# A hybrid layer's weight splits: one queue with steps four ticks apart, and row sums of a block loaded ahead

## The chip, the core and the metric

The kernel runs on one core of one Trainium2 chip. The metric is the device time of one execution in microseconds, the median of several runs. One further execution is recorded by the hardware profiler; all durations below that are called "profiled" come from it.

## The reference

One layer of a generator over 2048 tokens of width 1024, with 256 context tokens ahead of it. An input projection of 9216 columns feeds eight heads of a gated linear recurrence in both directions (query, value, two forget gates, output gate) and a gated short convolution of 1024 channels; one output projection follows, and a residual add and a norm.

```python
h = rmsnorm(x, norm_w[l]) * (1.0 + scale[:, None]) + shift[:, None]
p = h @ w_in[l]                                     # 2048 x 1024 @ 1024 x 9216
pc = hc @ (w_in[l, :, :HG_COLS] if last else w_in[l])   # 256 context rows, recurrence columns only
qc, vc, kcf, gcf, kcb, gcb = hgrn_prep(pc[..., :HG_COLS], lb_f, lb_b)
oc, s_f, s_b = bidir_scan(qc, kcf, kcb, vc, gcf, gcb, s0, s0)
q, v, kf, gf, kb, gb = hgrn_prep(p[..., :HG_COLS], lb_f, lb_b)
o, _, _ = bidir_scan(q, kf, kb, v, gf, gb, s_f, s_b)
y_hg = hgrn_out(o, p[..., 4 * HG_WIDTH:HG_COLS], hg_onorm_w[l], x.dtype)
y_cv = conv_branch(p[..., HG_COLS:], conv_w[l], grid=True)
y = jnp.concatenate([y_hg, y_cv], axis=-1) @ w_out[l]
```

`bidir_scan` runs the recurrence S_t = diag(f_t) S_{t-1} + k_t v_t^T, o_t = S_t^T q_t forwards and backwards. All of it is float32, so the kernel carries every matmul operand as two float16 parts, a high one and the remainder.

## The kernel before

**Units.** The input projection goes by *pairs* of 128 weight columns. A pair and a group of 512 tokens make a *unit* (`seven`, lines 881 to 925): seven products A11·B11, S1·T1, S2·T2, A12·B21, S3·T3, S4·B22, A22·T4 on half-size operands, each of three matmuls (high·high, high·low, low·high) in each of four steps. After every such step of three matmuls stands a *tick* (line 1372). A unit has 28 ticks. Its products collect in three PSUM banks, in the trace `sa`, `sb` and `sc`; ScalarE copies `sa`, `sb`, `sa` out after the first three products (`keep`, line 897), VectorE adds the later ones (`plus`, line 901). The last product, A22, is issued within the next unit, after that one's first.

**Order of work.** Each of eight heads has four windows of 512 tokens. A window has a unit of the *z pair* (the two gates' columns; p24 to p31 in names are the z pairs of heads 0 to 7), a unit of the *v pair* (value and query; p8 to p15), and in some windows a unit of a *gate pair* shared by two heads (p32, p34, p36, p38, with buffers of its own, `own=True`). The first window of a head has short context units too (8 ticks each). Then come four windows of the first convolution pairs (p56 and p48) and fourteen windows of pairs p57 to p63 and p49 to p55, in which a unit is 512 columns wide instead of 256. In between, at ticks set by a table of paces, stand the steps of the recurrence: multiplications of K, Q and tot by levels on VectorE, copies on ScalarE, small matmuls.

**Splitting a pair.** `load_pair` (line 364) makes the operands of a pair from two staged blocks of 128 x 1024 float32. Row sums: `sizes` (line 378, ScalarE, two activations) and their sum `rb` (382). `begin` (385) calls `pow2_scale`, which puts one 128x1 matmul `ss` on TensorE (line 139) that reads `rb`, and three tiny VectorE instructions that make the scale `sc`. Then come the splits (lines 151 and 152: ScalarE casts the high part, VectorE computes the remainder) of A11 with A12 in one instruction of 1024, of S1, A22, S2, S3, S4 in 512 each, and VectorE sums at 393, 404, 410 and 413 that make S1 to S4 in place.

**When it is split.** When the last use of a pair is over, `retire` calls `next_w(own, 4)`. It takes the block loaded ahead, or loads one, empties whatever of older pairs is still to be split (`flush`), and puts the new pair into `deferred` with a wait of four ticks. From then on `tick` (1372 to 1379) takes one step of the front pair at each tick: the two row sums, a gap of six ticks in the heads or two in the convolution (line 415), then the nine steps from `begin` to S4 at nine ticks in a row, and last a load of the next block (`load_ahead`). `settle` at a unit's start (line 1390) issues what is left of that unit's pair.

**What sets the order on an engine.** The program's order gives each instruction its priority; a scheduler then fills each engine's queue from what is ready by its own account. A step may so stand earlier in a queue than its tick says, and never waits for its tick on the chip: only the place in the queue counts, and each engine runs its queue in order.

## Time and profile before

| | us |
|---|---|
| median of 3 runs | 2182.38 |
| lowest and highest run | 2182.03, 2183.33 |
| the profiled execution | 2187.49 |
| its span, first to last instruction | 2185.7 |
| TensorE busy in the span | 2089.4 |
| VectorE busy | 1652.1 |
| ScalarE busy | 1169.2 |
| granted TensorE clock, mean | 0.99 |

The profiled execution took 1.8 us more than its span, and 5.1 us more than the median of the runs. A busy engine is one with an instruction in work; for TensorE the difference between span and busy time, 96 us, is the time in which it waited.

### The profile page before, as it was taken

Reading aid. Unit: us, or ns where it says so; the run is one execution under the profiler, and the core shown is the slowest. Engines: PE = TensorE matmul, PEld = TensorE weight load, DVE = VectorE, ACT = ScalarE, POOL = GpSimd, SP = SyncE. Lnnn points to the kernel's source line nnn. Section 1 sums busy time; section 2 is a strip of 40 time slices with the busy share of each in tenths; the row PEclk is TensorE's granted clock in tenths of the full one; section 3 lists DMA queues with packets and bytes.
Section 4 is the critical chain, followed back from the end, with each engine's and each line's share of the span. In section 5 each row is a group of like instructions: output and inputs, shape, how many; then the busy total and the mean of one; then the engine's idle time right before and its main releaser. Section 6 shows DMA issues by size and latency. Waiting matters only on the chain.

```text
span 2185.7 us, 51899 instructions
## 1 busy us (share of the span) xinstructions
PE 2089.4 (96%) x21563; PEld 1468.2 (67%) x21563; DVE 1652.1 (76%) x3456; ACT 1169.2 (53%) x2341; POOL 157.9 (7%) x239
## 2 busy tenths in 40 slices
PE   5789999999999999999999999999999999999998
PEld 2677688888887988888889887444444444444443
DVE  7887777878779778788687786677787656687775
ACT  7865556666557565666675654344444423333332
POOL 0211111010010110101111000000000000000000
PEclk9999999999999999999999999999999999999999
DMA  9766533433243333333633448923443205633321
GB/s 349 238 205 208 181 132 103 141 116 105 86 159 107 114 114 125 111 108 128 194 123 123 140 156 260 274 97 121 135 139 98 66 30 181 213 124 108 127 85 58
DMA packets 196464, 310.41 MB, mean 142 GB/s; under 512 B 13570, under 2 KB 126594, under 8 KB 194436
## 3 DMA queue, kind: packets, MB, share of 16 engines
q1 hardware_dynamic: 194068, 303.16, 42.5%
q8 instruction: 169, 2.77, 0.5%
q10 hardware_dynamic: 2160, 3.93, 0.5%
q14 instruction: 67, 0.55, 0.1%
HBM read 241.77 MB, written 65.27 MB: 140 GB/s over the span
## 4 chain that ended last, share of the span: by engine, by line
PE 66%; DVE 18%; ACT 8%; DMA 5%; issue 2%; POOL 1%; SPq 0%; POOLq 0%; ACTq 0%; DVEq 0%
PE sa L890 8%; PE sa L891 8%; PE sa L892 8%; PE sb L890 4%; PE sb L891 4%; PE sb L892 4%; PE sa_o L890 2%; PE sa_o L891 2%; PE sa_o L892 2%; DVE e_p L152 2%; PE A L599 2%; PE sc L890 2%; PE sc L892 2%; PE sc L891 2%; DVE K L453 2%
## 5 line engine op out<-in xcount | busy, mean ns | idle before, releaser
L453 DVE TENSOR_TENSOR K<-K,tot 128x512 f32<-128x512 f32 x192 | 133.6, 696 | 60.1 <-PE A L627 27.6
L891 PEld LDWEIGHTS <-e_p 128*128 128x128 f16 x1368 | 134.1, 98 | 60.4 <-issue 10.9
L890 PEld LDWEIGHTS <-e_p 128*128 128x128 f16 x1368 | 134.1, 98 | 59.9 <-DMA hop1T<-Hd1T 2.6
L892 PEld LDWEIGHTS <-e_p 128*128 128x128 f16 x1368 | 134.2, 98 | 52.8 <-issue 1.8
L460 DVE TENSOR_TENSOR Q<-Q,tot 128x512 f32<-128x512 f32 x192 | 132.4, 690 | 44.3 <-PE A L599 30.9
L569 ACT ACTIVATE km<-K 128x512 f32<-128x512 f32 x160 | 109.0, 686 | 69.5 <-DVE K L453 60.0
L890 PEld LDWEIGHTS <-whib_p 128*128 128x128 f16 x912 | 89.3, 98 | 41.2 <-issue 5.0
L890 PEld LDWEIGHTS <-whia_p 128*128 128x128 f16 x912 | 89.4, 98 | 38.5 <-DMA hop3B<-Hd3B 2.8
L891 PEld LDWEIGHTS <-whib_p 128*128 128x128 f16 x912 | 89.4, 98 | 38.2 <-issue 4.1
L891 PEld LDWEIGHTS <-whia_p 128*128 128x128 f16 x912 | 89.3, 98 | 37.7 <-issue 5.6
L892 PEld LDWEIGHTS <-wlob_p 128*128 128x128 f16 x912 | 89.4, 98 | 34.7 <-issue 0.5
L892 PEld LDWEIGHTS <-wloa_p 128*128 128x128 f16 x912 | 89.4, 98 | 34.4
L151 ACT ACTIVATE e_p<-ws_p,sc_p 128x512 f16<-128x512 f32 x108 | 77.2, 717 | 53.4 <-DVE ws_p L413 33.3
L576 POOL COPY qm<-Q 128x512 f32<-128x512 f32 x64 | 55.7, 870 | 630.2 <-DVE Q L460 627.2
L635 POOL COPY A<-Ac 32x128 f32<-32x128 f32 x128 | 68.3, 534 | 371.2 <-ACT A L631 367.2
L897 ACT ACTIVATE u<-sa,sx_w 128x256 f32<-128x256 f32 (+1 forms) x114 | 59.8, 525 | 59.2 <-PE sa L892 48.7
L897 ACT ACTIVATE p<-sb,sx_w 128x256 f32<-128x256 f32 (+1 forms) x114 | 59.4, 521 | 52.9 <-PE sb L892 52.3
L897 ACT ACTIVATE p<-sa,sx_w 128x256 f32<-128x256 f32 (+1 forms) x114 | 59.1, 518 | 47.4 <-PE sa L892 46.6
L152 DVE SCALAR_TENSOR_TENSOR e_p<-ws_p,sc_p,e_p 128x512 f16<-128x512 f32 x108 | 78.5, 742 | 1.0 <-ACT e_p L151 1.0
L813 ACT ACTIVATE cv<-c,small 128x512 f32<-128x512 f32 (+1 forms) x36 | 24.2, 674 | 97.6 <-DVE c L831 52.9
L378 ACT ACTIVATE junk<-ws_p 128x1024 f16<-128x1024 f32 x72 | 75.7, 1051 | 0.2
L151 ACT ACTIVATE hiS_o<-y_o,sc_y 128x1024 f16<-128x1024 f32 x32 | 36.8, 1149 | 72.6 <-PE sa_o L891 32.2
(865 smaller groups left out, 6972.1 us busy)
## 6 DMA issues: line engine op xcount, KB each, us to landing
ws_p<-in_w_in SPq DMA_DIRECT2D x72, 512.0 KB, 4.4
y_o<-yT SPq DMA_DIRECT2D x32, 512.0 KB, 4.2
xt_x<-in_x SPq DMA_DIRECT2D x16, 512.0 KB, 4.6
wa<-in_w_ada SPq DMA_DIRECT2D x16, 512.0 KB, 10.2
Gd<-zs SPq DMA_DIRECT2D x32, 256.0 KB, 3.2
...
```

Of the source, the lines that this page charges most:

```text
L151: S.activation(hi, src, AF.Copy, scale=st[:, 0:1])
L152: V.scalar_tensor_tensor(lo, src, st[:, 0:1], hi, ALU.mult, ALU.subtract)
L378: S.activation(junk.rearrange("p (k n) -> p k n", k=KT), stage[i], AF.Abs, accum_out=r)
L453: V.tensor_tensor(m, m, sub(cur, nb + 1, [[2, np_], [-(nb + 1), 2], [0, B]]), ALU.mult)
L460: V.tensor_tensor(m, m, sub(cur, 1, [[2, np_], [nb - 1, 2], [0, B]]), ALU.mult)
L569: S.activation(sub(s.km, 0, [[2 * B, n // (2 * B)], [B, 2], [1, B]]), mix(s.K, n, B, n // (2 * B)), AF.Copy)
L576: G.tensor_copy(sub(qm, 0, [[2 * B, n // (2 * B)], [B, 2], [1, B]]), mix(s.qf, n, B, n // (2 * B)))
L635: G.tensor_copy(A3[js, :, js], s.Ac[js])
L890: PE.matmul(ps, hi[:, k], rh, start=start and k == 0, stop=False, skip_group_check=not start)
L891: PE.matmul(ps, hi[:, k], right(name, 1, k), start=False, stop=False, skip_group_check=not start)
L892: PE.matmul(ps, lo[:, k], rh, start=False, stop=k == nk - 1, skip_group_check=not start)
L897: last_keep.append(S.activation(r, ps, AF.Copy, scale=sx))
```

## The change

`deferred`, a list of pairs with their steps, becomes `jobs`, a queue of generators. A tick counts down the wait of every job, and moves the front job alone by one step when its wait is over; a job that is finished leaves the queue. Nothing empties the queue any more but `settle`, and that only up to the pair that the unit needs.

- A pair's steps are parted into `pre` (the two row sums) and `rest` (the nine steps from `begin` to S4). Between two steps of `rest` stand `room` ticks: 4 for the heads' pairs, 3 and 2 for the first two convolution blocks, 1 after that.
- When a block has been loaded ahead, a job of its own is queued with a wait of 16 ticks, which takes its row sums two ticks apart. It stands behind the splits of the pair in front. When that pair's turn comes, its `pre` is empty, and it goes to `begin` without the gap.
- A gate pair is loaded when its job comes to the front (not when the older one retires), and 12 ticks later its row sums begin. The first gate pair, p32, so goes from `begin` at the fourth tick of window 1's z unit, with a step at every tick, to `begin` at the sixteenth tick, with one at every fourth.

The same instructions are issued; the changed kernel's line numbers are one higher from line 417 on (its copies of products are at 898). Matmuls of the products are untouched. By ticks, the nine steps of a z pair stay in the last window's v unit and the start of the gate unit behind it; those of the v pair move from the gate unit to the gate unit's end and the next head's first z unit; those of the gate pairs p34, p36 and p38 move from that z unit to the first v unit and the second window.

```diff
--- before.py
+++ after.py
@@ -412,10 +412,11 @@
         def sum_b():
             V.tensor_tensor(a12, a12, a11, ALU.subtract)
 
-        gap = 6 if col0 < 5 * HG else 2
-        w.rest = [lambda: behind(lambda: sizes(0)), lambda: behind(lambda: sizes(1))] + [lambda: None] * gap
-        w.rest += [begin, whole, part("S1", lambda: t["s1"]), sum_a, part("A22", lambda: a22),
-                   part("S2", lambda: a11), sum_b, part("S3", lambda: a21), part("S4", lambda: a12)]
+        w.pre = [lambda: behind(lambda: sizes(0)), lambda: behind(lambda: sizes(1))]
+        w.rest = [begin, whole, part("S1", lambda: t["s1"]), sum_a, part("A22", lambda: a22),
+                  part("S2", lambda: a11), sum_b, part("S3", lambda: a21), part("S4", lambda: a12)]
+        block = col0 // P - 5 * HEADS
+        w.gap, w.room = (6, 4) if block < 0 else (2, {0: 3, 1: 2}.get(block % 8, 1))
         return w
 
 
@@ -961,15 +962,13 @@
         load_C(ext.op, 0, OPS[6:])
         load_C(ext.op, 1, OPS)
 
-    deferred = []
-
-    def settle(w):
-        while w.rest:
-            w.rest.pop(0)()
-
-    def flush():
-        while deferred:
-            settle(deferred.pop(0)[1])
+    jobs = []
+
+    def settle(wk):
+
+        while any(j_[1] == wk for j_ in jobs):
+            for _ in jobs.pop(0)[2]:
+                pass
 
     def wo_scan(k):
         for j in range(2):
@@ -1266,6 +1265,8 @@
     ws = {}
 
     ahead, loaded = [], []
+    given = [0, 0]
+    in_order = [list(todo[0]), list(todo[1])]
 
     def load(own):
         wk = todo[own].pop(0)
@@ -1277,17 +1278,44 @@
 
         if todo[0] and not ahead and not loaded[-2].rest:
             ahead.append(load(0))
+            jobs.append([16, None, sizes_ahead(ahead[0])])
+
+    def sizes_ahead(w):
+        while w.pre:
+            w.pre.pop(0)()
+            yield
+            yield
+
+    def split_steps(own):
+
+        if ahead and not own:
+            w = ahead.pop()
+        else:
+            w = load(own)
+            yield from range(12)
+        load_ahead()
+        if w.pre:
+            while w.pre:
+                w.pre.pop(0)()
+                yield
+            yield from range(w.gap)
+        while w.rest:
+            w.rest.pop(0)()
+            yield from range(w.room)
+        load_ahead()
 
     def next_w(own, wait=0):
-        if todo[own] or (ahead and not own):
-            flush()
-            w = ahead.pop() if ahead and not own else load(own)
-            if wait:
-                w.rest.append(load_ahead)
-                deferred.append([wait, w])
-                load_ahead()
-            else:
-                settle(w)
+        if given[own] == len(in_order[own]):
+            return
+        wk = in_order[own][given[own]]
+        given[own] += 1
+        if wait:
+            jobs.append([wait, wk, split_steps(own)])
+        else:
+            w = load(own)
+            for f_ in w.pre + w.rest:
+                f_()
+            w.pre, w.rest = [], []
 
 
     hop = {}
@@ -1371,12 +1399,12 @@
 
         def tick(weight):
             pace[0] += weight
-            for d_ in deferred:
-                d_[0] -= 1
-            while deferred and not deferred[0][1].rest:
-                deferred.pop(0)
-            if deferred and deferred[0][0] <= 0:
-                deferred[0][1].rest.pop(0)()
+            for j_ in jobs:
+                j_[0] -= 1
+            if jobs and jobs[0][0] <= 0:
+                front = jobs[0]
+                if next(front[2], front) is front:
+                    jobs.remove(front)
             while not pending and pace[1] < len(steps) and steps[pace[1]][0] * total <= pace[0]:
                 steps[pace[1]][1]()
                 pace[1] += 1
@@ -1386,8 +1414,8 @@
             gw -= 1
         turnover = wi + 1 < len(group_of) and group_of[wi + 1] != group_of[wi]
         for un, (wk, kind, i, fn) in enumerate(units):
+            settle(wk)
             w = ws[wk]
-            settle(w)
             if not hasattr(w, "sx"):
                 finish_w(w, f"w{ui}")
             final = turnover and kind != "ctx" and all(u[1] == "ctx" for u in units[un + 1:])
```

**Head 1 to head 2, z pair p26, TensorE.** `ss_p26` is the scale's matmul; `sb`, `sc` and `sa` are products of the running unit, `A4` and `A5` small matmuls of the recurrence. Before:

```order
L892 MATMUL sc_26_5287<-hop7B21_4815,wloa_p9_3299 128x256
L139 LDWEIGHTS rb_p26_5268
L139 MATMUL ss_p26_5300<-rb_p26_5268 128x1
L617 MATMUL A5_1_1_5313<-Q_1_1_4972,K_1_1_4481 32x64 x16
L890 LDWEIGHTS e_p9_3302
L890 MATMUL sa_26_5166<-hop7T3_4848,e_p9_3302 128x256
```

After:

```order
L893 MATMUL sb_26_5210<-hop7T1_4513,wlob_p9_3325 128x256
L139 LDWEIGHTS rb_p26_3619
L139 MATMUL ss_p26_5227<-rb_p26_3619 128x1
L600 MATMUL A4_1_1_5240<-qm3_1_1_5191,km3_1_1_5145 32x32 x16
L600 MATMUL A4_1_1_5240<-Q_1_1_4978,km4_1_1_5194 32x32 x16
L891 LDWEIGHTS e_p9_3326
L891 MATMUL sa_26_5172<-hop7T2_4759,e_p9_3326 128x256
```

It stood behind the product A12 (`sc_26`) and stands behind S1 (`sb_26`), two products earlier, ahead of the S2 product (`sa_26<-hop7T2`).

**The same place, ScalarE.** `rsum` are p26's row sums, `whia`, `whib` and `e` the high parts of its splits, `p1`, `p5` and `u2` copies of products, `f`, `K` and `km` the recurrence. Before, ahead of the first split:

```order
L378 ACTIVATE junk_129,rsum_p260_5221<-ws_p260_3194 128x1024
L491 ACTIVATE f_1_0_4942<-f_1_0_4942,lb_136,lb1_137 128x512
L510 ACTIVATE f_1_0_4942<-sa_25_4944,sx_w16_3368 128x256
L492 ACTIVATE K_1_0_4943<-f_1_0_4942 128x512
L491 ACTIVATE f_1_0_4942<-f_1_0_4942,lb_136,lb1_137 128x512
L897 ACTIVATE p5_26_5261<-sb_26_5208,sx_w19_3715 128x256
L492 ACTIVATE K_1_0_4943<-f_1_0_4942 128x512
L378 ACTIVATE junk_129,rsum_p261_5266<-ws_p261_3196 128x1024
L897 ACTIVATE u2_26_5285<-sa_26_5166,sx_w19_3715 128x256
L569 ACTIVATE km0_1_0_5650<-K_1_0_4943 128x512
```

The row sums after the change stand in the first window of head 1, a head earlier:

```order
L898 ACTIVATE u2_16_3477<-sa_16_3358,sx_w16_3353 128x256
L378 ACTIVATE junk_129,rsum_p260_3609<-ws_p260_3312 128x1024
L378 ACTIVATE junk_129,rsum_p261_3617<-ws_p261_3314 128x1024
L512 ACTIVATE f_1_3_3356<-f_1_3_3356 128x256
L570 ACTIVATE km4_0_3_3602<-K_0_3_2633 128x512
```

and the splits:

```order
L493 ACTIVATE K_1_0_4949<-f_1_0_4948 128x512
L492 ACTIVATE f_1_0_4948<-f_1_0_4948,lb_136,lb1_137 128x512
L898 ACTIVATE p5_26_5278<-sb_26_5210,sx_w19_3721 128x256
L493 ACTIVATE K_1_0_4949<-f_1_0_4948 128x512
L151 ACTIVATE whia_p26_5233<-ws_p260_3312,sc_p26_5229 128x1024
L151 ACTIVATE whib_p26_5235<-s1_p26_5238,sc_p26_5229 128x512
L898 ACTIVATE u2_26_5301<-sa_26_5172,sx_w19_3721 128x256
L151 ACTIVATE whib_p26_5235<-ws_p261_3314,sc_p26_5229 128x512
L151 ACTIVATE e_p26_5237<-ws_p261_3314,sc_p26_5229 128x512
L570 ACTIVATE km0_1_0_5636<-K_1_0_4949 128x512
L151 ACTIVATE e_p26_5237<-ws_p260_3312,sc_p26_5229 128x512
L898 ACTIVATE p1_27_5420<-sa_27_5370,sx_w9_1688 128x256
```

The two row sums have left this place, and copies of products now stand between the splits.

**Head 2, gate pair p34, VectorE.** `wloa`, `wlob` and `e` are remainders, `ws` and `s1` the sums in place, `f_2_0` outputs of the z unit, `vT_2_0` and `q_2_0` of the v unit, `Q`, `K`, `Ac`, `ks` and `S` steps of the recurrence. Before, in the z unit:

```order
L460 TENSOR_TENSOR Q_1_0_5420<-Q_1_0_5420,tot_1_0_5648 128x64x2x4
L152 SCALAR_TENSOR_TENSOR wloa_p34_5744<-ws_p340_5625,sc_p34_5739,whia_p34_5743 128x1024
L152 SCALAR_TENSOR_TENSOR wlob_p34_5746<-s1_p34_5748,sc_p34_5739,whib_p34_5745 128x512
L410 TENSOR_TENSOR ws_p340_5625<-s1_p34_5748,ws_p340_5625 128x512
L152 SCALAR_TENSOR_TENSOR wlob_p34_5746<-ws_p341_5627,sc_p34_5739,whib_p34_5745 128x512
L413 TENSOR_TENSOR ws_p340_5625<-ws_p340_5625 128x512
L152 SCALAR_TENSOR_TENSOR e_p34_5747<-ws_p340_5625,sc_p34_5739,e_p34_5747 128x512
L607 COPY_PREDICATED Ac_1_0_5710<-mask_138,A2_1_0_5788 128x128
L152 SCALAR_TENSOR_TENSOR e_p34_5747<-ws_p341_5627,sc_p34_5739,e_p34_5747 128x512
L607 COPY_PREDICATED Ac_1_0_5710<-mask_138,A2_1_0_5788 128x128
L152 SCALAR_TENSOR_TENSOR e_p34_5747<-ws_p340_5625,sc_p34_5739,e_p34_5747 128x512
L901 SCALAR_TENSOR_TENSOR f_2_0_5593<-sb_28_5631,sx_w28_5590,u2_28_5722 128x256
```

After, in the v unit:

```order
L454 TENSOR_TENSOR K_1_0_4949<-K_1_0_4949,tot_1_0_5634 128x4x2x64
L461 TENSOR_TENSOR Q_1_0_5416<-Q_1_0_5416,tot_1_0_5634 128x4x2x64
L152 SCALAR_TENSOR_TENSOR wloa_p34_6026<-ws_p340_5858,sc_p34_6021,whia_p34_6025 128x1024
L902 SCALAR_TENSOR_TENSOR vT_2_0_5956<-sc_31_6036,sx_w31_5953,p1_31_5984 128x256
L152 SCALAR_TENSOR_TENSOR wlob_p34_6028<-s1_p34_6030,sc_p34_6021,whib_p34_6027 128x512
L902 SCALAR_TENSOR_TENSOR q_2_0_5957<-sa_31_5958,sx_w31_5953,p5_31_6005 128x256
L410 TENSOR_TENSOR ws_p340_5858<-s1_p34_6030,ws_p340_5858 128x512
L152 SCALAR_TENSOR_TENSOR wlob_p34_6028<-ws_p341_5860,sc_p34_6021,whib_p34_6027 128x512
L902 SCALAR_TENSOR_TENSOR vT_2_0_5956<-sb_31_5986,sx_w31_5953,u2_31_6034 128x256
L538 TENSOR_TENSOR ks_2_0_6158<-K_2_0_5579 128x512
L696 SCALAR_TENSOR_TENSOR S_1_0_3_6121<-S_1_1_0_5487,tot7_1_0_5635,T_1_01_6116 128x128
L152 SCALAR_TENSOR_TENSOR e_p34_6029<-ws_p340_5858,sc_p34_6021,e_p34_6029 128x512
```

Before, all of the pair's remainders stand between the second and the third output of the z unit; now they begin in the v unit, with an output or a step of the recurrence between most of them.

**The last convolution window, pair p57, VectorE.** `z1_0_3` is an output of the running unit whose bank the next product needs, `b0_0_3` another, `cv0` a sum of the convolution, `ymax` one of the heads' output. Before:

```order
L850 TENSOR_TENSOR cv0_0_3_21117<-b0_0_3_21205,cv0_0_3_21117 128x256
L152 SCALAR_TENSOR_TENSOR wloa_p57_21167<-ws_p570_19704,sc_p57_21162,whia_p57_21166 128x1024
L152 SCALAR_TENSOR_TENSOR wlob_p57_21169<-s1_p57_21171,sc_p57_21162,whib_p57_21168 128x512
L410 TENSOR_TENSOR ws_p570_19704<-s1_p57_21171,ws_p570_19704 128x512
L152 SCALAR_TENSOR_TENSOR wlob_p57_21169<-ws_p571_19706,sc_p57_21162,whib_p57_21168 128x512
L413 TENSOR_TENSOR ws_p570_19704<-ws_p570_19704 128x512
L152 SCALAR_TENSOR_TENSOR e_p57_21170<-ws_p570_19704,sc_p57_21162,e_p57_21170 128x512
L152 SCALAR_TENSOR_TENSOR e_p57_21170<-ws_p571_19706,sc_p57_21162,e_p57_21170 128x512
L152 SCALAR_TENSOR_TENSOR e_p57_21170<-ws_p570_19704,sc_p57_21162,e_p57_21170 128x512
L901 SCALAR_TENSOR_TENSOR z1_0_3_21227<-sa_113_21085,sx_w107_20135,p5_113_21142 128x256
```

After:

```order
L152 SCALAR_TENSOR_TENSOR wlob_p57_21155<-s1_p57_21157,sc_p57_21148,whib_p57_21154 128x512
L723 TENSOR_REDUCE ymax_139<-y_7_2_21189 128x1
L410 TENSOR_TENSOR ws_p570_19779<-s1_p57_21157,ws_p570_19779 128x512
L152 SCALAR_TENSOR_TENSOR wlob_p57_21155<-ws_p571_19781,sc_p57_21148,whib_p57_21154 128x512
L902 SCALAR_TENSOR_TENSOR b0_0_3_21205<-sc_113_21180,sx_w107_20141,p1_113_21127 128x256
L152 SCALAR_TENSOR_TENSOR e_p57_21156<-ws_p570_19779,sc_p57_21148,e_p57_21156 128x512
L851 TENSOR_TENSOR cv0_0_3_21123<-b0_0_3_21205,cv0_0_3_21123 128x256
L413 TENSOR_TENSOR ws_p570_19779<-ws_p570_19779 128x512
L902 SCALAR_TENSOR_TENSOR z1_0_3_21223<-sa_113_21091,sx_w107_20141,p5_113_21159 128x256
L152 SCALAR_TENSOR_TENSOR e_p57_21156<-ws_p571_19781,sc_p57_21148,e_p57_21156 128x512
L152 SCALAR_TENSOR_TENSOR e_p57_21156<-ws_p570_19779,sc_p57_21148,e_p57_21156 128x512
```

`z1_0_3` stood behind all nine steps and now has the last two remainders behind it.

## The prediction

> **What bounds the kernel now.** I read the page first. Columns of its second row: busy time, share of the span, instructions.
>
> ```profile
> span 2185.7 us, 51899 instructions
> PE 2089.4 (96%) x21563; PEld 1468.2 (67%) x21563; DVE 1652.1 (76%) x3456; ACT 1169.2 (53%) x2341; POOL 157.9 (7%) x239
> PE 66%; DVE 18%; ACT 8%; DMA 5%; issue 2%; POOL 1%; SPq 0%; POOLq 0%; ACTq 0%; DVEq 0%
> ```
>
> TensorE works 96% of the span and waits 96.3 us (2185.7 − 2089.4). The chain that ended last, third row, is TensorE's for two thirds. The change leaves every matmul of the products as it is, so it can only take time from those 96.3 us, add to them, or change the clock. Which of them wait on the splitting of pairs, or on a copy or output that may stand behind a split, is told by the waits of TensorE (columns: reader, releaser, us in total, times, longest):
>
> ```profile
> PE ss_p L139 <- DVE rb_p L382: 21.7, 12, 13.9
> PE sa L890 <- ACT p L897: 6.1, 8, 2.4
> PE A L599 <- DVE tot L466: 3.6, 3, 1.2
> ...
> PE sa L890 <- DVE z L901: 2.3, 1, 2.3
> ...
> PE sa L890 <- ACT u L897: 1.7, 5, 0.8
> ...
> PE sa L890 <- DVE f L901: 1.6, 1, 1.6
> ...
> PE A L599 <- ACT km L569: 0.9, 1, 0.9
> PE sc L890 <- ACT q L543: 0.9, 1, 0.9
> ```
>
> Then TensorE's own timeline, for when these waits come (start, length, instruction, and in brackets the wait ahead of it):
>
> ```profile
> 117.41 0.37 PE L890 MATMUL sa<-hop1B,whia_p 128*128 128x256 f16 x1 [1.56 <-DVE f L901]
> ...
> 220.43 0.18 PE L139 MATMUL ss_p<-rb_p 128*128 128x1 bf16 x1 [2.48 <-DVE rb_p L382]
> ...
> 374.14 0.27 PE L890 MATMUL sa<-hop7T,e_p 128*128 128x256 f16 x1 [0.58 <-ACT p L897]
> ...
> 691.94 0.18 PE L139 MATMUL ss_p<-rb_p 128*128 128x1 bf16 x1 [0.61 <-DVE rb_p L382]
> 702.26 0.46 PE L599 MATMUL A<-Q,km 128*32 128x32 f32 x32 [1.19 <-DVE tot L466]
> ...
> 1369.03 0.27 PE L890 MATMUL sa<-hop35T,whib_p 128*128 128x256 f16 x1 [2.34 <-DVE z L901]
> ...
> 1870.37 0.38 PE L890 MATMUL sa<-C1T,e_p 128*128 128x512 f16 x1 [2.36 <-ACT p L897]
> ```
>
> Out of reach are the 13.9 us at the start (the first pair's load, before any queue) and the 2.4 us at 1870 (in the output projection, after the last pair). What is in reach is 7.8 + 3.7 + 3.6 + 2.3 + 1.6 + 1.7 + 0.9 + 0.9 = 22.5 us, about 1% of the time. So this is a change of some ten microseconds at best, in either direction.
>
> **What splitting a pair costs.** Groups of VectorE's instructions by shape (last columns: busy in total, mean ns | idle before):
>
> ```profile
> L152 DVE SCALAR_TENSOR_TENSOR e_p<-ws_p,sc_p,e_p 128x512 f16<-128x512 f32 x108 | 78.5, 742 | 1.0 <-ACT e_p L151 1.0
> L152 DVE SCALAR_TENSOR_TENSOR wloa_p<-ws_p,sc_p,whia_p 128x1024 f16<-128x1024 f32 x36 | 46.1, 1282 | 12.9 <-ACT whia_p L151 12.9
> L152 DVE SCALAR_TENSOR_TENSOR wlob_p<-s_p,sc_p,whib_p 128x512 f16<-128x512 f32 x36 | 27.9, 774 | 0.0
> L152 DVE SCALAR_TENSOR_TENSOR wlob_p<-ws_p,sc_p,whib_p 128x512 f16<-128x512 f32 x36 | 26.8, 744 | 0.0
> L404 DVE TENSOR_TENSOR ws_p<-ws_p,ws_p 128x512 f32<-128x512 f32 x36 | 24.6, 684 | 0.1
> L410 DVE TENSOR_TENSOR ws_p<-s_p,ws_p 128x512 f32<-128x512 f32 x36 | 24.6, 683 | 0.0
> L413 DVE TENSOR_TENSOR ws_p<-ws_p 128x512 f32<-128x512 f32 x36 | 24.6, 682 | 0.0
> L393 DVE TENSOR_TENSOR s_p<-ws_p 128x512 f32<-128x512 f32 x36 | 24.5, 681 | 0.0
> ```
>
> They add to 277.6 us for 36 pairs, 7.7 us of VectorE a pair. At nine ticks in a row that is a burst; four ticks apart it is spread over 36 ticks, more than the 28 of a unit. The total stays. Where the room lies, the busy times of each engine show, in four stretches from head 3's last window on: its gate unit; the first z unit of head 4, with the burst of gate pair p36 in it; the v unit behind that; the z unit of the second window. Columns: stretch, length, PE, PEld, DVE, ACT, POOL busy, clock, DMA share, GB/s.
>
> ```profile
> 672.49:688.03 15.54, 15.31 (x192) 13.35 (x189) 15.54 (x33) 12.13 (x23) 0.60 (x1) 1.00 0.27 93
> 688.03:707.87 19.84, 17.80 (x299) 14.88 (x297) 19.20 (x45) 16.38 (x30) 1.84 (x2) 1.00 0.44 147
> 707.87:726.18 18.31, 18.29 (x177) 16.55 (x174) 16.12 (x43) 6.73 (x13) 2.14 (x4) 1.00 0.60 207
> 726.18:739.67 13.49, 13.49 (x239) 12.05 (x236) 7.79 (x18) 10.30 (x34) 0.66 (x1) 1.00 0.01 2
> ```
>
> VectorE is full in the gate unit (15.54 of 15.54) and nearly so in the z unit (19.20 of 19.84), yet TensorE loses only 0.23 and 2.04 us there: it runs ahead on three banks. The room is in the second window, 13.49 − 7.79 = 5.7 us.
>
> **The sum, gains first.** *a) The scale's matmul `ss_p`.* It stands in TensorE's queue and waits for `rb` (382), which waits for the row sums (378) in ScalarE's queue and then for its turn on VectorE. For z and v pairs the row sums now run a window or more ahead, so their waits vanish. Three waits of gate pairs (691.94 is one; 0.61 each, 1.8) keep their form: row sums, gap, `begin`. So 7.8 − 1.8 = 6.0. Bounds: 3.5 if a `rb` that comes early still queues behind VectorE's work at 220.43 for the 2.48 us it does now, 7.8 if the gate pairs go too.
>
> *b) Copies of `p` (897).* In the rows below the copy runs right behind a split that itself waited for a VectorE sum, and TensorE waited 0.58 for the copy.
>
> ```profile
> 373.01 0.72 ACT L151 ACTIVATE e_p<-ws_p,sc_p 128x512 f16<-128x512 f32 x1 [0.78 <-DVE ws_p L410]
> 373.64 0.46 ACT L897 ACTIVATE p<-sa,sx_w 128x256 f32<-128x256 f32 x1
> ```
>
> With the splits begun two products earlier that sum is done in time, and copies stand between the splits. Of 6.1 − 2.4 = 3.7 us I take 3.0 (bounds 0 and 3.7).
>
> *c) `tot` (466) in the z unit.* It is late because a gate pair's burst stands ahead of it on VectorE (702.26 is in p36's z unit). Its 7.7 us leave this unit, but by the order some two thirds of a v pair's come in. I take 2.4 of 3.6 (bounds 0 and 3.6).
>
> *d) Pair p57 at 1369.* `z1` stood behind nine steps of which VectorE had these ahead of it at the end:
>
> ```profile
> 1366.51 2.07 DVE L152 SCALAR_TENSOR_TENSOR e_p<-ws_p,sc_p,e_p 128x512 f16<-128x512 f32 x3
> 1368.49 0.48 DVE L901 SCALAR_TENSOR_TENSOR z<-sa,sx_w,p 128x256 f32<-128x256 f32 x1
> ```
>
> Two of the three `e` now follow it, so it comes some 1.4 us sooner, and a sum or so more since the start is earlier: 1.7 of 2.3. The clock fell behind this wait:
>
> ```profile
> 222.00:226.00 4.00, 4.00 (x30) 2.02 (x27) 4.00 (x13) 2.11 (x4) 0.76 (x1) 1.00 0.96 282
> ...
> 1366.00:1370.00 4.00, 1.66 (x12) 1.04 (x10) 3.98 (x9) 1.22 (x3) 0.00 (x0) 0.92 0.20 56
> 1370.00:1374.00 4.00, 4.00 (x17) 2.00 (x16) 3.00 (x9) 2.09 (x4) 0.00 (x0) 0.65 0.87 303
> ```
>
> At 0.65 for 4.00 us and 0.92 for 1.66, TensorE lost 0.35 × 4.00 + 0.08 × 1.66 = 1.5 us. That comes back if the wait shrinks, so d) is 1.7 + 1.5 = 3.2 (bounds 0 and 3.8). After the 2.48 us at 220 the clock stayed at 1.00 (first row), so a gap of that size does not always cost it. [...]
>
> *e) `f` at 117.* The first gate pair p32 had its burst ahead of these outputs; now it begins twelve ticks later. 0.8 of 1.6 (bounds −1.6, if the outputs at its new place wait alike, and 1.6).
>
> *f) `u`, `km`, `q`: 3.5 us together.* Each stands in a queue with splits; which of them a spread burst frees I cannot tell. 1.5 (bounds 0 and 3.5).
>
> Gains: 6.0 + 3.0 + 2.4 + 3.2 + 0.8 + 1.5 = 16.9.
>
> **What it adds.** *g) Gate pairs in the v unit.* By the order on VectorE p34's remainders now begin ahead of that unit's first output. Its nine steps reach past the unit's end, so up to 7.7 − 0.7 = 7.0 us come on top of 16.1: 23.1 in a unit of 18.31, 4.8 too many. The outputs wait behind them on VectorE, and TensorE waits for the outputs' banks. The 5.7 us free in the next unit take up the backlog. The z unit shows the price of such a load: 19.20 of VectorE against 17.80 of TensorE, 1.4 over, cost 2.04. The gate unit, 0.23 over, cost 0.23. Spread steps let the outputs through between them, so I take 1.2 for each of p34, p36 and p38, 3.6 in all; bounds 0 (backlog carried) and 3 × 4.8 = 14.4.
>
> *h) Row sums of a block loaded ahead, in ScalarE's queue.*
>
> ```profile
> L378 ACT ACTIVATE junk<-ws_p 128x1024 f16<-128x1024 f32 x72 | 75.7, 1051 | 0.2
> ...
> ws_p<-in_w_in SPq DMA_DIRECT2D x72, 512.0 KB, 4.4
> ```
>
> They take 2 × 1.05 us and wait for a load of 4.4 us. For z pairs the load has long landed; for p11, p13 and p15, and the gate pairs, the row sums stand a few ticks behind it (a tick is 13.49 / 28 = 0.5 us), and copies wait behind them in ScalarE's queue. TensorE has two banks in hand meanwhile. I take 1.0 (bounds 0 and 3.0). SP issues the same loads at nearly the same places.
>
> Sum: 16.9 − 3.6 − 1.0 = 12.3 us off the profiled 2187.5, 2175.2. The profiled execution lies 5.1 above the median, so **2170 us**, 0.56% faster.
>
> **Rivals.** Measurements of this kernel tell apart about 0.2%, 4.4 us: faster is below 2178.0, slower above 2186.7.
>
> *R1, slower: VectorE becomes the bound of z and v units of the three heads with gate pairs.* Before they hold 19.2 + 16.1 = 35.3 us of VectorE in 38.15; after, with the v pair's two thirds (5.1) in place of 7.7 in the first, and 7.0 more in the second, 39.7, against 36.1 of TensorE's work. If the v unit takes VectorE's time with the z unit's slack of 0.64, it lasts 23.7, 5.4 more than 18.31, and each such stall costs the clock 1.5 as at 1369: 3 × 6.9 = 20.7. Then c) brings nothing either. 20.7 + 1.0 − 14.5 = 7.2 slower: 2190. It decides from 14.5 − 1.0 + 4.4 = 17.9 us over three units, 6 us each. For it: the sum of 39.7. Against it: z units already live at 97% for 2 us, and banks and the free next unit soften it. Chance 0.13.
>
> *R2, no change: the waits pass on.* TensorE is ahead of VectorE where these waits fall, so a freed `ss_p` or copy lets it run into the next output. Then a) gives its low 3.5, d) 1.7, b), c), e), f) nothing; 3.6 and 1.0 are paid: 0.6 off, 2182. For it: VectorE full in both units above. Against it: most `ss_p` waits come while three banks are free. Chance 0.18.
>
> *R3, all 22.5 us and the clock's 1.5 go, and nothing is added:* 2187.5 − 24.0 − 5.1 = 2158. For it: work left on VectorE is the same and only its lumps go. Against it: the gate pairs' `ss_p`. Chance 0.13.
>
> **How the numbers follow.** My forecast 2170 has 0.56, with its own range of 2163 to 2177. Half of R3 and nearly all of R2 (2177 to 2185) are taken in with 2158 to 2184; what is left out is R1 and half of R3, near 0.2. Faster: 0.56 + 0.13 and a little of R2, 0.70. Within 0.2%: R2's rest and a little of R1, 0.18. Slower: 0.12.
>
> **What the profile after would show.** a) TensorE's waits for `rb_p` at about 15.5 to 16, the start's 13.9 and the gate pairs' 0.6 left; the row sums of z and v pairs well ahead of their `ss_p`. b) Waits for `p` at about 3. c) `tot` below 1.5. d) No wait above 1 us near 1369 and a clock of 1.00 behind it. g) In v units after a gate pair's load, lengths of 19 to 20 us, with new waits for outputs (`vT`, `q`) of 1 us or so; R1 has 23 and more there. R2 shows `rb_p` as forecast, and new waits for outputs or copies of the same size. R3 shows neither. The forecast is wrong if the sum of TensorE's waits falls by less than 5 us or by more than 20, or if its busy time changes by more than the clock's 1.5.

## The result

| | median us | lowest to highest | ratio to the kernel before, 95% interval |
|---|---|---|---|
| before, 6 runs | 2182.86 | 2181.98 to 2188.05 | |
| changed, 6 runs | 2172.26 | 2168.64 to 2176.29 | 0.9940 [0.9927, 0.9953] |

The change saves 10.6 us by the medians, 0.5%; the ratio, over all runs, says 0.6%. The forecast was 2170. The reasons behind it held less well than the number: the largest term was not gained where the text had it, one term hardly came at all, and one new wait was not foreseen. From the page of the changed kernel:

```profile
span 2169.3 us, 51904 instructions
PE 2082.1 (96%) x21563; PEld 1467.7 (68%) x21563; DVE 1644.1 (76%) x3456; ACT 1166.1 (54%) x2341; POOL 168.5 (8%) x239
```

TensorE's waits fell from 96.3 to 87.2 us (2169.3 − 2082.1), and its busy time from 2089.4 to 2082.1 with the same 21563 matmuls. Its waits (reader, releaser, us in total, times, longest):

```profile
PE ss_p L139 <- DVE rb_p L382: 14.4, 2, 14.1
...
PE gate_r L1046 <- DMA wg<-in_w_ada: 4.6, 1, 4.6
...
PE A L600 <- DVE Q L461: 4.3, 9, 2.0
...
PE oT L792 <- DVE y L794: 2.4, 1, 2.4
PE vt_c L524 <- ACT vT_c L519: 2.2, 3, 0.8
PE T L652 <- DVE y L794: 2.2, 5, 0.4
PE sa L891 <- DVE f L902: 2.1, 6, 0.4
PE sb L891 <- DVE b L902: 1.9, 1, 1.9
```

The waits for `rb_p` are gone but for the start, those for `tot`, for `z` and (but for 0.8 us in the output projection) for `p` too. Others stand in their place: those for `oT`, `vt_c`, `T` and `b` are new, `wg`'s has grown from 1.7 and that for `Q` from 2.0, and `f`'s comes six times instead of once. (`gate_r` was at line 1047 before: the numbers are one higher only as far as line 961.) A list of waits does not say which of them were exchanged for which. For that I cut both traces at the same matmuls, and compared lengths. First the heads: from the first product of a head's second window to that of the next head's, seven stretches, of which the first, third and fifth hold a gate pair's split at the head's turn. Two of the seven rows and the sum, before and then after (stretch, length, PE, PEld, DVE, ACT, POOL busy, clock, DMA share, GB/s):

```profile
427.64:572.91 145.27, 143.40 (x2115) 126.36 (x2113) 112.37 (x250) 87.05 (x197) 15.19 (x24) 1.00 0.35 112
572.91:720.90 147.99, 144.12 (x2116) 126.30 (x2114) 119.48 (x266) 93.01 (x207) 15.83 (x24) 1.00 0.37 121
...
sum 1011.30, PE 988.72 PEld 867.70 DVE 801.09 ACT 635.43 POOL 108.50; mean PE 141.25 PEld 123.96 DVE 114.44 ACT 90.78 POOL 15.50
```

```profile
422.75:568.30 145.55, 143.22 (x2115) 126.21 (x2113) 115.32 (x262) 88.17 (x199) 17.78 (x24) 1.00 0.36 117
568.30:713.77 145.47, 143.62 (x2115) 126.38 (x2113) 114.32 (x254) 91.48 (x205) 18.21 (x24) 1.00 0.36 118
...
sum 1001.17, PE 985.67 PEld 867.89 DVE 794.88 ACT 634.97 POOL 122.01; mean PE 140.81 PEld 123.98 DVE 113.55 ACT 90.71 POOL 17.43
```

The heads give 10.1 us. The three stretches with a gate pair give 9.2 of them (436.8 to 427.6, the sums of their lengths); the four without give 0.9 (574.5 to 573.6). A stretch without one is not faster at all in the rows shown (145.27 and 145.55), though its waits of 0.49 us for `rb_p` and 0.58 for `p` are gone. The rest of the program, cut likewise (from the first product on, the rest of head 0, the passage to the convolution, the passage to the output projection):

```profile
97.06:190.25 93.19, 83.38 (x1092) 71.22 (x1091) 79.27 (x176) 59.52 (x109) 19.30 (x28) 0.93 0.58 190
190.25:286.86 96.61, 88.03 (x1146) 69.41 (x1144) 73.94 (x167) 53.36 (x100) 11.65 (x17) 1.00 0.69 223
1324.17:1411.96 87.79, 81.14 (x529) 51.93 (x527) 54.01 (x109) 34.99 (x70) 0.00 (x0) 0.98 0.89 259
...
1866.55:1896.66 30.11, 27.75 (x122) 12.18 (x120) 19.12 (x28) 10.11 (x13) 0.00 (x0) 0.94 0.82 281
```

```profile
97.56:188.69 91.13, 80.57 (x1092) 68.23 (x1091) 78.40 (x178) 63.86 (x118) 19.14 (x28) 0.98 0.62 194
188.69:285.34 96.65, 87.29 (x1146) 69.79 (x1144) 74.43 (x167) 53.62 (x100) 10.21 (x17) 0.96 0.69 223
1312.51:1400.02 87.51, 81.01 (x529) 52.23 (x527) 52.17 (x107) 33.45 (x68) 0.00 (x0) 0.98 0.86 252
...
1853.37:1880.22 26.85, 26.06 (x121) 11.73 (x120) 17.58 (x26) 9.09 (x12) 0.00 (x0) 1.00 0.93 317
```

So −2.1, 0.0, −0.3 and −3.3 us; with −10.1 in the heads, and −1.2 and +0.5 elsewhere, they make the profiles' difference of 16.4 (2185.7 − 2169.3). The last, 3.3, is not the change's: it is the wait of 2.36 us for `p` at 1870 and the clock behind it, 0.50 for 3.41 us (1871.14 to 1874.55). A wait for `p` of 2.4 to 2.9 us is present in four of this study's fourteen profiles (before, and the runs called `nosums`, `late` and `best2` below) and absent from ten, whatever their splits. The 3.3 us are most of the 5.1 us by which the profile of before lay above its median. Without it the profiles differ by 13.1.

### The profile page after: what moved, and what is told of

The parts are those of the page before. It is cut to its first block, busy times and chain, and to the rows that moved or that the text cites. A ratio compares the mean times of both kernels' runs of the same rounds, so it can differ in the third digit from the quotient of the medians.

```text
span 2169.3 us, 51904 instructions
## 1 busy us (share of the span) xinstructions
PE 2082.1 (96%) x21563; PEld 1467.7 (68%) x21563; DVE 1644.1 (76%) x3456; ACT 1166.1 (54%) x2341; POOL 168.5 (8%) x239
## 4 chain that ended last, share of the span: by engine, by line
PE 68%; DVE 16%; ACT 6%; DMA 5%; issue 3%; SPq 1%; POOL 1%; POOLq 0%; ACTq 0%; DVEq 0%
PE sa L891 8%; PE sa L893 8%; PE sa L892 8%; PE sb L891 4%; PE sb L893 4%; PE sb L892 4%; PE sa_o L891 2%; PE sa_o L893 2%; PE sa_o L892 2%; PE sc L891 2%; PE A L600 2%; PE sc L893 2%; PE sc L892 2%; DVE K L454 2%; DVE Q L461 2%
## 5 line engine op out<-in xcount | busy, mean ns | idle before, releaser
L636 POOL COPY A<-Ac 32x128 f32<-32x128 f32 x128 | 82.2, 642 | 366.2 <-ACT A L632 274.8
L151 ACT ACTIVATE e_p<-ws_p,sc_p 128x512 f16<-128x512 f32 x108 | 76.0, 716 | 26.3 <-DVE ws_p L413 14.5
L378 ACT ACTIVATE junk<-ws_p 128x1024 f16<-128x1024 f32 x72 | 75.6, 1051 | 18.1 <-DMA ws_p<-in_w_in 17.7
```

What stands on the lines that cost most here:

```text
L151: S.activation(hi, src, AF.Copy, scale=st[:, 0:1])
L378: S.activation(junk.rearrange("p (k n) -> p k n", k=KT), stage[i], AF.Abs, accum_out=r)
L636: G.tensor_copy(A3[js, :, js], s.Ac[js])
```

## The experiments

Twelve kernels, all made from the changed one, each timed against the kernel before:

| run | what differs from the changed kernel | median us | ratio to before, 95% interval |
|---|---|---|---|
| `after2` | nothing | 2170.88 | 0.9948 [0.9929, 0.9968] |
| `room1` | heads' steps at every tick | 2202.48 | 1.0091 [1.0061, 1.0120] |
| `nosums` | no row sums ahead | 2181.58 | 0.9991 [0.9982, 1.0001] |
| `late` | row sums 40 ticks after the load | 2202.88 | 1.0092 [1.0077, 1.0107] |
| `gap8` | first step eight ticks later | 2169.60 | 0.9936 [0.9920, 0.9952] |
| `room1_gap8` | both `room1` and `gap8` | 2183.72 | 0.9999 [0.9989, 1.0009] |
| `skip58` | no row sums ahead for p58 | 2171.47 | 0.9945 [0.9929, 0.9962] |
| `best1` | `skip58`, gate matmuls in head 1 | 2177.96 | 0.9974 [0.9962, 0.9986] |
| `own4` | `room1_gap8`, gate pairs spread | 2181.07 | 0.9977 [0.9967, 0.9986] |
| `own1` | `gap8`, gate pairs at every tick | 2175.06 | 0.9949 [0.9934, 0.9964] |
| `conv1` | convolution's steps at every tick | 2176.31 | 0.9956 [0.9942, 0.9970] |
| `best2` | `skip58` and `gap8` in the heads | 2167.05 | 0.9921 [0.9906, 0.9936] |

**The same kernel again.**

> The changed kernel itself, a second time. Theory (the gain is real and sits in TensorE's waits): 2168 to 2176 us; in its profile waits for rb_p near 14.4 us, none for tot, new ones for gate_r (4.6), for y at the oT transposition (2.4) and for b in the first convolution pair windows (1.3 and 1.9). Rival (the new waits are chance of one execution): gate_r, y and b are below 1 us each here, and other waits stand elsewhere.

Measured: `gate_r` 4.7, `y` 2.1, `b` 1.3 and 1.3, `rb_p` 14.5; one wait of 1.4 for `tot`, in head 0, was not expected. The new waits belong to the kernel, not to one execution. This second profile also shows how far two executions of one kernel differ: its passage to the convolution took 85.62 us instead of 87.51, its heads 998.8 instead of 1001.2.

**Each half alone.** `room1` puts the heads' steps back to one at every tick; `nosums` leaves out the row sums ahead.

```diff
-        w.gap, w.room = (6, 4) if block < 0 else (2, {0: 3, 1: 2}.get(block % 8, 1))
+        w.gap, w.room = (6, 1) if block < 0 else (2, {0: 3, 1: 2}.get(block % 8, 1))
```

> The changed kernel with the nine steps of the heads' pairs at nine ticks in a row; queue, row sums ahead and the gate pairs' later load stay. Theory (two separate gains: row sums ahead take away the waits for rb_p, the spread takes away those for p and tot): rb_p stays near 14.4 us, p and tot come back by 4 to 7 us, 2175 to 2179 us. Rival 1 (the spread does everything): rb_p comes back too, 2180 us or more. Rival 2 (row sums ahead do everything): 2170 to 2174 us.

```diff
             ahead.append(load(0))
-            jobs.append([16, None, sizes_ahead(ahead[0])])
```

> The changed kernel without the row sums of blocks loaded ahead: they are taken in the pair's own turn, with the gap of six ticks before its first step, the spread stays. Theory (two separate gains): rb_p comes back by 3 to 6 us, p and tot stay away, ScalarE's wait for loads at its row sums (17.7 us) goes, 2174 to 2178 us. Rival 1 (the spread does everything): 2170 to 2174 us, rb_p near 14.4. Rival 2 (row sums ahead do everything): 2180 us or more.

`room1` was 32 us slower than the changed kernel (2202.5 and 2170.9), 18 slower than before; no theory had that. The waits for `rb_p` stayed away, as both the theory and rival 2 had it, but another came, five times in the heads' turns, each 2.67 us. Its place at 682 in TensorE's timeline, and VectorE's ahead of it:

```profile
682.30 0.68 PE L628 MATMUL A<-Q,K 128*64 128x64 f32 x14 [2.68 <-DVE Q L461]
```

```profile
678.97 1.40 DVE L152 SCALAR_TENSOR_TENSOR e_p<-ws_p,sc_p,e_p 128x512 f16<-128x512 f32 x2
680.30 0.68 DVE L454 TENSOR_TENSOR K<-K,tot 128x512 f32<-128x512 f32 x1
680.90 0.74 DVE L152 SCALAR_TENSOR_TENSOR e_p<-ws_p,sc_p,e_p 128x512 f16<-128x512 f32 x1
681.56 0.68 DVE L461 TENSOR_TENSOR Q<-Q,tot 128x512 f32<-128x512 f32 x1
```

The level's `Q` stands behind the last remainders of a pair in VectorE's queue. Since the row sums are done, a pair starts eight ticks sooner, and a burst now meets this level. Five of the seven stretches have a clock of 0.99 there, against 1.00 in all seven of the changed kernel's. So `room1` changed two things: burst and place.

`nosums` lost nearly all of the gain: 2181.6 instead of the 2174 to 2178 expected, as rival 2 had it, which `room1` contradicts. Its waits for `rb_p` came back by 5.1 (19.5 in all), but the larger part is one that nobody had listed:

```profile
PE ss_p L139 <- DVE rb_p L382: 19.5, 9, 13.8
PE A L600 <- ACT km L570: 11.6, 8, 1.5
```

`km` is a copy on ScalarE. Its eight waits, 11.6 us, are more than the 8.4 us by which the seven stretches are longer than the changed kernel's (1009.6 and 1001.2). ScalarE reaches `km` late; whether the two row sums (2.1 us) that are back in the head's turn do that, or the place of the high parts spread into it, this run does not tell.

**Burst, place and row sums apart.** `gap8` waits, where the row sums are done, the eight ticks that they and the gap would take; `room1_gap8` does so with bursts, which stand then near the places of before (the table below has them).

```diff
             yield from range(w.gap)
+        else:
+            yield from range(2 + w.gap)
```

> The changed kernel with row sums ahead and steps four ticks apart, but a pair whose row sums are done still waits the ticks that they and the gap would take (8 in the heads, 4 in the convolution) before its first step, as in the kernel without row sums ahead (2181.6 us). Theory A (the row sums' place in ScalarE's queue costs: beside them the copies km come late): waits for rb_p near 14.4 us, for km below 2, 2169 to 2175 us. Theory B (what counts is that the first step comes eight ticks sooner): km is waited for as without row sums ahead (11.6 us), 2177 to 2182 us.

> The same later first step, with the nine steps of the heads' pairs at nine ticks in a row: the burst back at the ticks of the kernel before, row sums ahead. Theory A (a burst hurts by where it falls; eight ticks sooner it met the levels of Q and K, which cost 20 us and more): waits of the levels for Q back to the 2 to 5 us of the kernel before, rb_p near 14.4, p and tot waited for again, 2176 to 2181 us. Theory B (a burst in this queue is bad wherever it falls): 2190 us or more.

The place matters for bursts above all: eight ticks later they cost 19 us less (2202.5 and 2183.7), while the spread steps stay the same (2170.9 and 2169.6). (Both also start the convolution's pairs four ticks later.) Theory A is right for `gap8` in the time and in `rb_p`; of `km`'s 11.6 us 4.6 remain, where it had below 2. In `room1_gap8` the levels' waits for `Q` fell back from 21.5 us to 6.9, most of the way, but the time did not follow and lies between the two theories: row sums ahead without the spread are worth nothing, 0.9999 of before. The head stretches, lengths summed by kind, and where the first remainder of the v pair and of the gate pair p36 stands in the third stretch (us from its start; the z pair's is at 90 or 91 in all four):

| splits | row sums | v pair | gate pair | three with a gate pair | four without | median us |
|---|---|---|---|---|---|---|
| burst (before) | in turn | 106.6 | 121.7 | 436.8 | 574.5 | 2182.86 |
| burst (`room1_gap8`) | ahead | 107.1 | 125.6 | 434.3 | 574.6 | 2183.72 |
| spread (`nosums`) | in turn | 112.4 | 139.1 | 431.2 | 578.3 | 2181.58 |
| spread (`gap8`) | ahead | 116.0 | 141.4 | 424.8 | 574.0 | 2169.60 |

Neither half is worth more than 2.5 us over the seven stretches; both together give 12.5 (1011.3 to 998.8), nearly all of it where a gate pair is split. There the spread alone gives 5.6, and it loses 3.9 at the four other turns. (The changed kernel's two profiles differ by 0.8 and 1.5 in these two sums.) What stands in the way when one half is missing, at the same turn, in `room1_gap8` and then in `nosums`:

```profile
703.59 0.27 PE L891 MATMUL sa<-hop15B,whia_p 128*128 128x256 f16 x1 [1.31 <-ACT f_c L497]
707.31 0.65 PE L618 MATMUL A<-Q,K 128*32 128x64 f32 x32 [0.61 <-DVE Q L461]
```

```profile
664.91 0.18 PE L139 MATMUL ss_p<-rb_p 128*128 128x1 bf16 x1 [0.49 <-DVE rb_p L382]
701.47 0.46 PE L600 MATMUL A<-Q,km 128*32 128x32 f32 x32 [1.53 <-ACT km L570]
```

`rb_p` and `tot` were the waits at which TensorE happened to stand first. With the row sums ahead and the burst left, it stands at the next operands instead; with the burst out of the way and the row sums in turn, at `km` on ScalarE.

That the spread is needed is shown by `room1_gap8`. That the row sums' own work is the other half is not, because their ticks also move the v pair. The wait for `km` follows the v pair's place. In the second to the sixth stretch of all kernels with spread steps, it is there (1.53 to 1.56 us) wherever the v pair's first remainder comes 111.5 to 113.8 us into the stretch, and nowhere when it comes by 110.6 or at 116.0. `nosums` has it at each of these turns, but so have `gap8`, `own1` and `best2`, with row sums ahead, at the turns without a gate pair; in `gap8`:

```profile
549.05 0.46 PE L600 MATMUL A<-Q,km 128*32 128x32 f32 x32 [1.53 <-ACT km L570]
```

No run has row sums in turn with the v pair at another place, so the two stay unseparated.

**Which pairs' bursts.** `own4` is `room1_gap8` with the gate pairs alone spread, `own1` is `gap8` with the gate pairs alone in a burst.

```diff
-            yield from range(w.room)
+            yield from range(4 if own else w.room)     # own4; in own1: 1 if own else w.room
```

> The kernel with row sums ahead and bursts at the ticks of the kernel before (2183.7 us), but the gate pairs' steps four ticks apart. Compared by the stretches from one head's second window to the next's: those with a gate pair took 139.9, 147.1 and 147.3 us with bursts and 136.8, 144.0 and 144.0 with all spread. Theory A (the gate pair's burst is what costs): these three fall by 2 to 3 us each, 2174 to 2178 us. Theory B (the bursts of the z and v pairs at the same turn cost, the gate pair's is covered by the second window): they stay within 0.7 us of the bursts' values, 2181 to 2185 us.

> The reverse: the kernel with the later first step (2169.6 us), all spread but the gate pairs, whose nine steps stand at nine ticks in a row in the v unit. Theory A: the three stretches with a gate pair rise by 2 to 3 us each, 2175 to 2179 us. Theory B: they stay within 0.7 us, 2168 to 2172 us. The forecast's price of a full v unit (1.2 us each, at most 4.8) would lie between.

The third stretch, with gate pair p36: `room1_gap8`, then `own4`, then `gap8`, then `own1`, of which the stretch behind it is shown too.

```profile
575.24:722.36 147.12, 143.26 (x2116) 126.23 (x2114) 119.11 (x266) 92.92 (x207) 15.72 (x24) 1.00 0.36 120
```

```profile
574.23:720.62 146.39, 143.26 (x2116) 126.26 (x2114) 118.54 (x264) 92.82 (x207) 16.41 (x24) 1.00 0.36 119
```

```profile
569.83:713.83 144.00, 142.83 (x2115) 126.33 (x2113) 113.07 (x253) 91.64 (x205) 16.80 (x24) 1.00 0.36 117
713.83:859.70 145.87, 143.23 (x2115) 126.35 (x2113) 118.02 (x263) 88.89 (x199) 16.68 (x24) 1.00 0.36 119
```

```profile
576.35:720.37 144.02, 142.84 (x2116) 126.35 (x2114) 113.08 (x253) 91.66 (x205) 16.84 (x24) 1.00 0.36 117
720.37:867.19 146.82, 143.62 (x2114) 126.34 (x2112) 117.90 (x263) 88.77 (x199) 17.23 (x24) 1.00 0.37 118
```

Spreading the gate pairs alone takes 0.75, 0.73 and 0.09 us off the three stretches, not 2 to 3; spreading the z and v pairs as well takes 7.9 more (432.7 to 424.8). Theory A falls: the form of the gate pair's split, burst or spread, is the smaller part. In the median, and within 0.05 us in the stretches, `own4` came out as theory B had it. That the bursts of the z and v pairs are what costs does not follow, since the gate pair waits in the queue behind the v pair, and a spread v pair moves it: p36's first remainder comes 125.6 us into the stretch in `own4` and 141.4 in `gap8`.

```profile
699.87 1.28 DVE L152 SCALAR_TENSOR_TENSOR wloa_p<-ws_p,sc_p,whia_p 128x1024 f16<-128x1024 f32 x1 [1.96 <-ACT whia_p L151]
```

```profile
711.21 1.28 DVE L152 SCALAR_TENSOR_TENSOR wloa_p<-ws_p,sc_p,whia_p 128x1024 f16<-128x1024 f32 x1
```

At the four turns without a gate pair, spreading the z and v pairs takes off 0.6 us in all (574.6 to 574.0). So the 7.9 may as well be the gate pair's move out of the z unit; no run moves it alone. The gate pair's burst in `own1` costs nothing in the stretch in which its split begins, and 1.0, 1.0 and 0.7 us in the one behind, since by then the second window has begun: a place that neither theory named. The medians rank alike (2175.1 against 2169.6, the first at the lower bound of theory A), but their intervals overlap, and the three stretches with a gate pair are the same (424.9 and 424.8). Whether the z pair's or the v pair's burst weighs more was not taken apart.

**ScalarE waiting for loads.** In the changed kernel ScalarE waits four times for a load at its row sums, 17.7 us in all, the longest in the convolution:

```profile
1393.25 1.06 ACT L378 ACTIVATE junk<-ws_p 128x1024 f16<-128x1024 f32 x1 [10.97 <-DMA ws_p<-in_w_in]
```

TensorE's wait of 1.85 us for `b` at 1396 follows it. `late` takes all row sums ahead 40 ticks after the load instead of 16; `skip58` leaves out p58's alone, which this row is.

```diff
-            jobs.append([16, None, sizes_ahead(ahead[0])])
+            jobs.append([40, None, sizes_ahead(ahead[0])])
```

> The changed kernel with the row sums of a block loaded ahead 40 ticks after the load instead of 16. Theory (ScalarE's 17.7 us of waiting for loads holds up copies, and TensorE waits for them): ScalarE's wait falls below 4 us, TensorE's wait for b at the second of the convolution's pair windows (1.9 us) and for f at the head turns (0.6) goes, 1.5 to 3 us less than the changed kernel. Rival (ScalarE's wait is covered by the banks): the wait falls the same, TensorE's waits stay, no change in time.

```diff
+            first_pair = todo[0][0][0] == 58 * P
             ahead.append(load(0))
-            jobs.append([16, None, sizes_ahead(ahead[0])])
+            if not first_pair:
+                jobs.append([16, None, sizes_ahead(ahead[0])])
```

> The changed kernel without row sums ahead for one pair, p58, for whose load ScalarE waited 10 to 11 us in the convolution. Theory (copies stand behind that wait): ScalarE's wait goes, TensorE's wait for b at that place (1.3 to 1.9 us) goes, 1 to 3 us less than the changed kernel in the profile. Rival (covered by the banks): TensorE's waits in that window stay within 0.5 us.

`late` took ScalarE's waits away as expected, and was 32 us slower than the changed kernel, which neither the theory nor the rival had. Of the 33.1 us between the two profiles, 23.4 lie in the convolution behind the passage, where its waits were these:

```profile
PE sc L891 <- DVE c L836: 9.2, 6, 1.9
...
PE sa L893 <- DVE wloa_p L152: 5.8, 6, 1.0
PE sa L891 <- ACT whia_p L151: 4.5, 6, 0.8
```

The queue moves its front job alone. A job that waits 40 ticks at the front holds up the splits of the next pair behind it; TensorE then waits for the operands themselves, once a window. In the heads, where TensorE does not come to wait for them, taking ScalarE's waits away changed no stretch by more than 0.7 us, but for the last (138.4 instead of 137.0), so there they are covered. In `skip58` the wait for `b` at 1396 is gone and the passage to the convolution took 86.67 us instead of 87.51. These 0.8 us are less than the 1.9 between the two profiles of the changed kernel, and the medians cannot show them either.

**The bursts of the convolution.**

```diff
-        w.gap, w.room = (6, 4) if block < 0 else (2, {0: 3, 1: 2}.get(block % 8, 1))
+        w.gap, w.room = (6, 4) if block < 0 else (2, 1)
```

> The changed kernel with one tick between the steps of the first two convolution blocks instead of three and two. Theory (the burst of p57 held back z and cost 2.3 us and 1.5 of clock, the spread passed this on to y and b): in the stretch from 1325 to 1416 us TensorE's waits are within 1.5 us of the changed kernel's, no change in time, 2168 to 2174 us. Rival (the spread is worth its 3 us there): z's wait of 2 us or more is back with a clock below 0.7 behind it, 3 us more.

```profile
1314.63:1405.09 90.46, 82.68 (x529) 52.43 (x527) 53.70 (x109) 34.54 (x70) 0.00 (x0) 0.96 0.87 252
```

```profile
1359.58 0.58 PE L891 MATMUL sa<-C0B,whia_p 128*128 128x512 f16 x1 [3.37 <-DVE b L902]
```

The passage took 90.46 us instead of 87.51, or 85.62 in `after2`: the rival is right in the size, 2.9 to 4.8 us, and the wait is `b`'s instead of `z`'s. In these profiles the spread is worth 3 to 5 us there, against a burst at this queue's ticks; part of it is the clock (0.96, against 0.98 in the changed kernel's profile; 0.58 in the 4 us behind this wait for `b`), and the intervals of the medians overlap. Against the kernel before (87.79) the changed one gains 0.3 or 2.2.

**Two versions meant to be faster.** `best1` also moves the gate matmuls (lines 1033 to 1053), for which TensorE waits 4.6 us at 228, two windows later, behind a head's turn.

```diff
-        if wi == NG - 1:
+        if wi == 5:
             extra = extra + gate_sums()
```

> The same as the run without p58's row sums ahead, and the eight gate matmuls with their loads moved from window 3 of head 0 to window 1 of head 1, where no store of the norms stands ahead of their loads on SP. Theory (the wait of 4.6 us for wg and the half clock behind it are lost in full): TensorE's wait for wg falls below 1 us, 5 to 8 us less than the changed kernel, 2162 to 2167 us. Rival (the wait is passed on to the vector work beside it): wg's wait goes, others in heads 0 and 1 grow by as much, 2169 to 2173 us.

It came out some 6 us higher than the changed kernel, and its waits for `wg` fell to 3.1 us only, in six pieces. The 9.3 us of TensorE's work on the gates came into the first head stretch (busy 144.69 instead of 135.38), which grew by 14.1:

```profile
282.00:433.48 151.48, 144.69 (x2064) 118.67 (x2062) 110.85 (x249) 90.16 (x200) 18.31 (x24) 1.00 0.42 135
```

while the rest of head 0 (from 190 on), from which they were taken, got shorter by less: 90.33 us instead of 96.65, 95.79 and 100.26 in the changed kernel, `after2` and `skip58`. The 14.1 are these 9.3 and new waits beside them. The wait for `wg` is real, and yet its removal by moving the work costs more than it.

```diff
+        elif w.gap == 6:
+            yield from range(8)
```

> The changed kernel with two edits that did no harm alone: the first step of the heads' pairs eight ticks later, and no row sums ahead for p58. Theory (the two act at different places): waits for b in the convolution below 1 us and for y, f at the head turns as in the run with the later step, 2164 to 2168 us. Rival (both were covered): 2169 to 2172 us.

`best2` has the lowest median, 2167.05, inside the theory's range, and is faster than before by 0.64% to 0.94%. Against the changed kernel its interval overlaps both of that kernel's, so that it beats this one is not shown; the wait for `b` at 1396 is gone, the other of 1.3 us stays, and the head stretches are those of `gap8`.

## Why the prediction was right, and where it was not

The time, the sign and the total of the waits (−9.1 us, foreseen between −5 and −20) came as forecast. Term by term:

- **a) `ss_p`, 6.0 forecast.** The waits fell by 7.6 us but for the start, more than forecast (one of 0.6 at 1253 stays, with another releaser): the gate pairs' three of 0.6 went too, where the text had them stay. But the step "their waits vanish, so 6.0 is gained" failed. In the stretches without a gate pair 0.49 us of `rb_p` and 0.58 of `p` went, and 0.43 of `y` and 0.45 of `f` came, in three of them also 0.70 to 0.77 of `vt_c`, right behind a turn with a gate pair, whose v unit the cut divides; the stretch is as long as before. Nor do all row sums run a window ahead: the z pairs' do, but those of head 4's v pair end at 671.3, 1.6 us before their `ss` at 672.9. The largest, 2.48 us at 220, went into the wait for `wg` behind it, 1.7 before and 4.6 now, with the clock at 0.58 for the next 4 us; 190 to 287 took 96.61 and takes 96.65. For these parts R2 (the waits pass on) was right.
- **b) and c), 3.0 and 2.4 forecast.** The waits for `p` (3.7) and `tot` (3.6) went entirely. What the three stretches with a gate pair gained, 9.2 us, is more than their `tot`, `p` and `rb_p` together: 3.6, 1.8 and 3.3 add to 8.7, and TensorE's busy time there fell too (144.12 to 143.62). c)'s picture, the gate pair's 7.7 us gone from the z unit, is not refuted and not shown: spreading the gate pair in place (`own4`) gives 1.6, and what moves it also spreads the z and v pairs.
- **d) p57, 3.2 forecast, 0.3 measured over the passage (2.2 in `after2`).** `z` comes sooner, as argued, and its 2.3 us are gone. But the step did not name what is late next: `b` waits 1.28 us at 1354 and 1.85 at 1396, and the stall that VectorE has there for a load (8.16 us before, 7.71 now) stands elsewhere in the queue, so that TensorE meets it at `oT` instead of at `c` (2.91 us before, with a clock of 1.00 over the next 4 us), now with a clock of 0.50 from 1341.13 to 1344.54:

```profile
1341.36 1.11 PE L792 MATMUL oT<-ident,Q 128*128 128x128 f32 x4 [2.40 <-DVE y L794]
```

- **e) and f), 0.8 and 1.5 forecast.** From 97 to 190 the gain was 2.1, but not in waits, which rose from 9.8 to 10.6 us; busy time fell by 2.8, with the clock at 0.98 instead of 0.93. `f` (1.56) went, but where p32's remainders now stand (112 to 132) there are now waits of 1.44 for `qm`, 1.97 for `Q` and 1.23 for `q`, nearer to the low bound of e) than to its 0.8. Of f), `q` and `km` went (0.9 each), and `u` grew from 1.7 to 2.6.
- **g) full v units, 3.6 forecast, about 2.2 measured.** The two units behind the turn and the second window's z unit, after:

```profile
681.99:700.75 18.76, 17.82 (x300) 14.95 (x297) 12.68 (x27) 14.32 (x30) 1.77 (x2) 1.00 0.39 129
700.75:719.81 19.06, 18.29 (x176) 16.55 (x176) 18.93 (x47) 10.70 (x19) 2.57 (x4) 1.00 0.72 248
719.81:733.43 13.62, 13.62 (x238) 12.04 (x236) 10.05 (x28) 10.42 (x34) 0.66 (x1) 1.00 0.01 1
```

  The z unit fell from 19.84 to 18.76 and its VectorE from 19.20 to 12.68; the v unit rose from 18.31 to 19.06, within the 19 to 20 named, and VectorE in it from 16.12 to 18.93. The sum of both, 39.7 by the text, is 31.6. The text let the whole gate pair but one remainder run in the v unit and two thirds of a v pair in the z unit; VectorE holds 2.8 us more in the one, and 6.5 less in the other. R1 stood on that sum, and falls with it. The wait in the v unit is for `vT_c` (2.2 us, three times), a copy on ScalarE, not for the outputs that the text named.
- **h) row sums behind loads, 1.0 forecast.** ScalarE waited 17.7 us; TensorE paid 0.6 at 692 and 1.85 at 1396, about 2.4, inside the bounds. The place, p58, was not among those named.
- **The profile's distance from the median.** The text took 5.1 us for a property of the profile. 3.3 of it is one wait at 1870 that comes and goes; the changed kernel's profiled execution, 2171.1, lies 1.2 below its median. The subtraction was needed, for a reason that was not given.
- **TensorE's busy time** was to change by no more than the clock's 1.5 us; it fell by 7.3, of which 3.1 in the head stretches at a clock of 1.00 throughout and with the same matmuls. By the text's own sign the forecast was wrong in this. So busy time holds waiting too, and the 22.5 us in reach were too few.

The forecast was right in total because too much gain in a), d) and e) stood against too much cost in g) and too little gain in the turns with a gate pair: a sum of eight terms whose errors went both ways. That it met the median within 2.3 us is in good part luck.
